# Attention keys turned by VectorE where they are normed, and loaded from DRAM already turned

## The chip, the cores and the metric

The kernel runs on one core of a Trainium2 chip. The time is that of the device, in microseconds, from runs of the whole program; the profile and the trace come from one profiled execution. The engines are called as in the profile: PE (TensorE, with PEld for its weight loads), DVE (VectorE), ACT (ScalarE), POOL (GpSimd) and SP (SyncE, which here issues nearly all DMAs). Each engine runs its instructions in the order in which they were written for it; a waiting instruction holds up all behind it on its engine.

## What is computed

One layer of a decoder: 1024 tokens, width 1024, float32. Half of the mixer is attention with eight heads in two key groups, over compressed, selected and windowed keys; the other half is a gated short convolution. A squared-ReLU MLP follows.

```python
h = rms_norm(x, g_mix_norm[l])
z = h @ w_in[l]
q, kc, vc, ks_, vs_, kw_, vw_, gl, hc, cg, bg = jnp.split(z, offs, axis=-1)
...
k_slc = rms_norm(ks_.reshape(kv_shape), g_k[l, 1])
k_win = rms_norm(kw_.reshape(kv_shape), g_k[l, 2])
...
attn_out = nsa_attention(q, k_cmp, v_cmp, k_slc, vs_.reshape(kv_shape),
                         k_win, vw_.reshape(kv_shape), gates)
conv_out = short_conv_mixer(hc, cg, bg, conv_w[l])
mixed = jnp.concatenate([rms_norm(attn_out, g_out[l, :ATTN_WIDTH]),
                         rms_norm(conv_out, g_out[l, ATTN_WIDTH:])], axis=-1)
x = x + mixed @ w_o[l]
h = rms_norm(x, g_ffn_norm[l])
x = x + jnp.square(jax.nn.relu(h @ w_up[l])) @ w_down[l]
```

The change concerns `k_slc` and `k_win`, the selected and the windowed keys: 1024 tokens by two groups of 64 each.

## The kernel before

**One plan for all engines.** Every operation is first recorded in a `Plan`. A list scheduler with a table of costs then puts the records of each engine in an order, the table `MOVES` sets some of them ahead of others by hand, and only then are they written out, all by one helper line (L268). So the order on an engine is not that of the source, and a record more or less renumbers those behind it: `MOVES` names records by number. `plan.drag` multiplies the size that the scheduler reckons for a DMA.

**Precision.** Products are built from float32 numbers split in two: a rounded high part and the rest, as in `KH` and `KL` for the keys, `hTh` and `hTl` for activations, `wcuh` and `wcul` for weights. ACT makes the high part and DVE or POOL the low one.

**Stages in time.** Norms and transposes of the input (0 to 28 us); products with the columns of `w_in` for keys, values, queries and gates (`zp`, to 150 us) with the compression MLP between (`hp`); convolution channels (`zX`, `zZ`, `zW`, 141 to 264 us), a Strassen-like scheme; the product with `w_o` for the convolution half (`wc`, from 264 us), with which the first scores (`s_`) are interleaved; attention (to 590 us); the MLP (`Z`, `X`, `W`, `Y`, to the end).

**The keys.** `k_norm(src, br, tb)` runs for each of eight token blocks and two branches: branch 1 (selected) from 31 to 73 us, branch 2 (windowed) from 134 to 157 us. DVE norms a block into `krow` (128 tokens by two groups by 64), and SP stores it twice, side by side, into `k_d[br]`, which lies in DRAM by tokens, in 256-byte pieces. At 257 us SP loads it back in four loads `kn`. `k_transposes` then turns it on PE: 32 transposes `tp<-ident,kn` into eight PSUM tiles. `split_keys` makes `KH` from each tile on ACT and `KL` on DVE, with the keys' 64 dimensions along the partitions, as the scores need them. `KH[g]` holds the high parts of a group twice, in both halves of the partitions; `KL` holds the low parts of both groups. Half of the transposes stand ahead of the `wc` groups, the others between them.

**Buffers.** `krow` comes from the pool `zt` with two buffers. A tile of the third k_norm waits until the first one's stores have landed. The weights of the convolution stage come in loads `wcr`, which ACT scales by the norm's gain (`wcr<-wcr,cols`, four pieces) and splits (`wcuh`); DVE makes `wcul`. Before the change the first `w_o` weights, residual rows (`y3`, `y2`, ...), `kn`, queries (`qx`) and values (`vs`, `vw`) are loaded between 256 and 275 us.

## Time and profile before

| | |
|---|---|
| median of 3 runs | 1213.78 us (1213.2 to 1215.11) |
| span of the profiled execution | 1212.3 us, 1.5 us below the median |
| PE busy | 1202.0 us, 99% of the span |
| 32 transposes of keys | 266.4 to 290.7 us, 272 ns median duration |
| eight `KH` and eight `KL` operations from PSUM | 598 and 688 ns median |
| `krow` stores | 32, 64 KB each, 586 ns of SP each, landing after 2.3 us (median) |
| DVE busy, 125 to 150 us | 22.30 of 25 us |
| DMA, 260 to 275 us | 354 to 372 GB/s |

A profile row of the timeline gives the start, the duration, the engine, the operation with its output and inputs, and in brackets the idle time ahead of it with what ended it. A duration on PE is a latency: matmuls follow one another more closely, 0.23 us for 512 columns and about 0.11 us for 128. What the engine spends is read from the distance between starts.

### The profile page before, as it was taken

To read this page: it belongs to the slowest core of one execution; us is meant where nothing else is said; L and a number is where in the kernel's file an instruction comes from. 1 tells how busy PE (TensorE), PEld (TensorE's weight loads), DVE (VectorE), ACT (ScalarE), POOL (GpSimd) and SP (SyncE) were. 2 spreads that over 40 slices of the span, in tenths; PEclk is the share of its full clock that TensorE was granted. 3 is DMA by queue.
4 is the path that set the end of the run, shared out by engine and by line. 5 is a ranking of instruction groups with operands and counts; after the bars stand their busy time and mean duration, and the time that the engine had idled before them with its cause. 6 is when DMAs were issued, how large, how long until landed. Compare 5 with 4: busy or idle time off the path is not lost.

```text
span 1212.3 us, 18361 instructions
## 1 busy us (share of the span) xinstructions
PE 1202.0 (99%) x5991; PEld 997.8 (82%) x5991; DVE 917.1 (76%) x1786; ACT 719.7 (59%) x1586; POOL 707.2 (58%) x629
## 2 busy tenths in 40 slices
PE   9999999999999999999999999999999999999998
PEld 6888977778888888888788888888888888888887
DVE  7957867684787898988866556555658898888885
ACT  7577855551588888778856556455335444444441
POOL 2444400011255545335859877777789999989971
PEclk9999999999999999999999999999999999999999
DMA  6375522265121200002234553535539555543513
GB/s 249 79 206 168 169 77 52 60 206 178 42 82 36 70 20 17 28 18 71 87 122 155 176 173 122 182 109 171 190 138 401 163 167 166 177 145 113 175 51 139
DMA packets 104360, 156.06 MB, mean 129 GB/s; under 512 B 20229, under 2 KB 58457, under 8 KB 104265
## 3 DMA queue, kind: packets, MB, share of 16 engines
q1 hardware_dynamic: 98000, 147.06, 37.0%
q10 hardware_dynamic: 5496, 5.28, 1.3%
q0 software_dynamic: 768, 2.56, 0.7%
q8 instruction: 47, 0.77, 0.3%
q14 instruction: 49, 0.39, 0.1%
HBM read 106.63 MB, written 48.23 MB: 128 GB/s over the span
## 4 chain that ended last, share of the span: by engine, by line
PE 93%; ACT 3%; DVE 3%; DMA 1%; issue 1%; POOL 0%; ACTq 0%; DVEq 0%; POOLq 0%
PE X L268 28%; PE Z L268 18%; PE zp L268 9%; PE tp L268 6%; PE zX L268 5%; PE ot L268 5%; PE wa L268 4%; PE W L268 4%; PE wc L268 3%; PE zZ L268 3%; PE zW L268 1%; PE hp L268 1%; ACT ph L268 1%; ACT wu L268 1%; PE tpq L268 0%
## 5 line engine op out<-in xcount | busy, mean ns | idle before, releaser
L268 PE MATMUL X<-we,uu 128*128 128x512 f32 x720 | 202.3, 389 | 0.0
L268 PE MATMUL Z<-we,uu 128*128 128x512 f32 (+1 forms) x582 | 169.1, 387 | 0.0
L268 PEld LDWEIGHTS X<-we,uu 128*128 128x128 f32 x720 | 135.1, 188 | 28.1
L268 ACT ACTIVATE uu<-ur 128x512 fp32r<-128x512 f32 x108 | 66.5, 630 | 116.8 <-PE Z L268 58.3
L268 PEld LDWEIGHTS Z<-we,uu 128*128 128x128 f32 x582 | 108.6, 188 | 22.4
L268 ACT ACTIVATE pt<-pt,nm 128x640 f32<-128x640 f32 (+7 forms) x128 | 93.7, 735 | 17.5 <-DVE nm L268 17.5
L268 PE MATMUL tp<-ident,pt 128*128 128x128 f32 x528 | 102.4, 272 | 0.2
L268 DVE TENSOR_TENSOR y<-X,y 128x512 f32<-128x512 f32 x128 | 86.2, 684 | 20.6 <-PE X L268 20.1
L268 POOL TENSOR_TENSOR d<-d 128x512 f32<-128x512 f32 x64 | 96.1, 1522 | 9.6 <-DVE d L268 7.5
L268 DVE TENSOR_TENSOR pl<-tp,ph 128x512 fp32r<-128x512 f32 (+1 forms) x148 | 94.7, 653 | 7.3 <-ACT ph L268 6.9
L268 ACT ACTIVATE ph<-tp 128x512 fp32r<-128x512 f32 (+1 forms) x148 | 82.4, 575 | 28.5 <-PE tp L268 26.0
L268 DVE TENSOR_TENSOR y<-Z,y 128x512 f32<-128x512 f32 (+1 forms) x97 | 65.3, 679 | 27.1 <-PE Z L268 26.9
L268 POOL TENSOR_TENSOR uu<-ur,uu 128x512 fp32r<-128x512 f32 x54 | 82.3, 1530 | 0.9 <-ACT uu L268 0.7
L268 PEld LDWEIGHTS tp<-ident,pt 128*128 128x128 f32 x528 | 68.5, 140 | 10.5 <-POOL pt L268 0.6
L268 DVE TENSOR_TENSOR we<-s,we 128x512 fp32r<-128x512 f32 x42 | 41.2, 982 | 47.5 <-PE Z L268 19.0
L268 ACT ACTIVATE we<-s 128x512 fp32r<-128x512 f32 x55 | 34.7, 631 | 65.0 <-PE Z L268 36.5
L268 ACT ACTIVATE we<-wu 128x512 fp32r<-128x512 f32 x57 | 36.1, 636 | 54.4 <-PE X L268 39.7
L268 POOL TENSOR_TENSOR we<-wd,we 128x512 fp32r<-128x512 f32 x32 | 52.1, 1628 | 25.1 <-ACT we L268 24.9
L268 POOL IOTA d_sw<- 128x640 f32 (+1 forms) x2 | 1.2, 610 | 107.9 <-PE zZ L268 107.9
L268 DVE TENSOR_TENSOR we<-wu,we 128x512 fp32r<-128x512 f32 x38 | 49.2, 1297 | 18.2 <-PE X L268 9.9
L268 PE MATMUL zp<-w_lo,hTh 128*128 128x512 f32 (+1 forms) x192 | 62.9, 363 | 0.0
L268 POOL TENSOR_TENSOR pt<-pt,rr 128x640 f32<-128x640 f32 (+4 forms) x64 | 62.3, 1004 | 0.0
(1337 smaller groups left out, 3738.3 us busy)
## 6 DMA issues: line engine op xcount, KB each, us to landing
u_d<-d SPq DMA_DIRECT2D x112, 256.0 KB, 4.0
ur<-u_d SPq DMA_DIRECT2D x108, 256.0 KB, 2.8
wu<-in_w_up_dram SPq DMA_DIRECT2D x16, 1024.0 KB, 5.9
wd<-in_w_down_dram SPq DMA_DIRECT2D x16, 1024.0 KB, 7.0
xt<-in_x_dram SPq DMA_DIRECT2D x10, 512.0 KB, 5.4
w_raw<-in_w_in_dram SPq DMA_DIRECT2D x8, 512.0 KB, 5.3
w1r<-in_w_cmp_dram SPq DMA_DIRECT2D x16, 256.0 KB, 2.9
q_d<-qn SPq DMA_DIRECT2D x8, 512.0 KB, 5.1
```

Of the source, the lines that this page charges most:

```text
L268: getattr(engine, method)(*[real(x) for x in a], **{k: real(x) for k, x in kw.items()})
```

## The change

`k_norm` makes the split and the turn itself. ACT copies `krow` rounded into the first half of `kn`, POOL subtracts for the second half, and one DVE instruction turns the 128x256 tile in blocks of 32x32 into `kT`. Four stores, one for each 32 tokens, put it into `k_d[br]`, which now lies by dimension: 128 rows of high parts and 128 of low ones, 1024 tokens in a row. A store moves 32 KB in 256 pieces of 128 bytes. `kn` and `kT` have two buffers each.

Gone are the four loads of `kn`, the 32 transposes, and the eight operations each on ACT and DVE. In their place stand 20 loads on SP: 16 of 64x512 into the halves of `KH`, four of 128x512 into `KL`. The loads of `V` now stand behind them in the source. `MOVES` is renumbered, and has 22 entries fewer, 87 instead of 109; those that are gone name records of the first 350 us. [...]

```diff
-    k_d = [dram.tile([T, G * 2 * HD], F32, name=f"k_d{br}") for br in range(2)]
+    k_d = [dram.tile([2 * P, T], F32, name=f"k_d{br}") for br in range(2)]
...
-            kd = k_d[br - 1][tb * P:(tb + 1) * P].rearrange("p (g a d) -> p g a d", g=G, a=2)
-            for a in range(2):
-                nc.sync.dma_start(kd[:, :, a], dst)
+            kn = zt.tile([P, 2, G * HD], F32R, name="kn")
+            kT = zt.tile([P, 8, 32], F32, name="kT")
+            row = dst.rearrange("p g d -> p (g d)")
+            copy_act(kn[:, 0], row)
+            tt(nc.gpsimd, kn[:, 1], row, kn[:, 0].bitcast(F32), ALU.subtract)
+            nc.vector.transpose(kT.rearrange("p c i -> p (c i)"), kn.rearrange("p a n -> p (a n)").bitcast(F32))
+            kd = k_d[br - 1].rearrange("(c j) t -> j c t", j=32)
+            plan.drag = 2.7
+            for a in range(4):
+                t = tb * P + 32 * a
+                nc.sync.dma_start(kd[:, :, t:t + 32], kT[32 * a:32 * a + 32])
+            plan.drag = 1.0
...
-        kn = {}
-        for qd in range(2):
-            for br in range(2):
-                kn[br, qd] = y_tile([P, 4, G, 2 * HD], f"kn{br}{qd}")
-                nc.sync.dma_start(kn[br, qd].rearrange("p t g d -> p t (g d)"),
-                                  k_d[br][qd * 512:(qd + 1) * 512].rearrange("(t p) n -> p t n", p=P))
...
+        for qd in range(2):
+            for br in range(2):
+                t = slice(qd * 512, (qd + 1) * 512)
+                c = slice(NCMP + br * T + qd * 512, NCMP + br * T + (qd + 1) * 512)
+                for g in range(G):
+                    for h_ in half:
+                        nc.sync.dma_start(KH[g][h_, c].bitcast(F32), k_d[br][half[g], t])
+                nc.sync.dma_start(KL[:, c].bitcast(F32), k_d[br][P:, t])
...
-        def k_transposes(g, br, qd):
-            tp = psP.tile([P, 4, P], F32, name="tp", tag="pt")
-            for j in range(4):
-                nc.tensor.transpose(tp[:, j], kn[br, qd][:, j, g], ident)
-            c0 = NCMP + br * T + qd * 512
-            split_keys(g, c0, 512, tp.rearrange("p a b -> p (a b)"))
...
-        kts = [(i % 2, i // 2 % 2, i // 4) for i in range(8)]
-        for i in range(4):
-            k_transposes(*kts.pop(0))
...
-            for i in range(2):
-                if kts:
-                    k_transposes(*kts.pop(0))
...
-    nc = _bacc.Bacc("TRN2", target_bir_lowering=False, num_devices=1)
+    nc = _bacc.Bacc("TRN2", target_bir_lowering=False, num_devices=1, dynamic_dma_scratch_size=8192)
```

**Where the order moves, first place: the convolution stage at about 161 us.** PE, before; the numbers behind names are those of records, and `wcuh_2213` and `wcul_2217` are the weight tile that the product `zX_2078` opens with:

```order
L268 MATMUL zW_2005<-hTh0_173,wcul_2046 128x512
L268 MATMUL zX_1882<-hTh1_124,wcul_2156 128x512
L268 MATMUL zZ_1972<-hTh1_124,wcuh_2152 128x512
L268 MATMUL zZ_1972<-hTl1_123,wcuh_2152 128x512
L268 MATMUL zZ_1972<-hTh1_124,wcul_2159 128x512
L268 MATMUL zZ_1972<-hTh1_124,wcuh_2152 128x512
L268 MATMUL zZ_1972<-hTl1_123,wcuh_2152 128x512
L268 MATMUL zZ_1972<-hTh1_124,wcul_2159 128x512
L268 MATMUL zX_2078<-hTh0_173,wcuh_2213 128x512
```

The same place of PE after the change, where that tile is `wcuh_2305` with `wcul_2329`:

```order
L268 MATMUL zW_2108<-hTh0_173,wcul_2134 128x512
L268 MATMUL zX_1994<-hTh1_124,wcul_2180 128x512
L268 MATMUL zX_2175<-hTh0_173,wcuh_2305 128x512
L268 MATMUL zX_2175<-hTl0_172,wcuh_2305 128x512
L268 MATMUL zX_2175<-hTh0_173,wcul_2329 128x512
L268 MATMUL zX_2175<-hTh0_173,wcuh_2305 128x512
L268 MATMUL zX_2175<-hTl0_172,wcuh_2305 128x512
L268 MATMUL zX_2175<-hTh0_173,wcul_2329 128x512
L268 MATMUL zX_2175<-hTh0_173,wcuh_2305 128x512
L268 MATMUL zZ_2066<-hTh1_124,wcuh_2251 128x512
```

ACT at the same place, before:

```order
L268 ACTIVATE ca_2171<-zZ_1972 128x512
L268 ACTIVATE wcuh_2209<-wcr_1731 128x512
L268 ACTIVATE wcr_2182<-wcr_2182,cols_64 128x256
L268 ACTIVATE wcuh_2213<-wcr_1732 128x512
L268 ACTIVATE wcr_2182<-wcr_2182,cols_64 128x256 x3
```

And ACT after the change, with the last `kn` copy of k_norm ahead:

```order
L268 ACTIVATE wcuh_2251<-wcr_1767 128x512
L268 ACTIVATE kn_2208<-krow_2196 128x128
L268 ACTIVATE wcuh_2298<-wcr_1767 128x512
L268 ACTIVATE wcr_2232<-wcr_2232,cols_64 128x256 x4
L268 ACTIVATE wcuh_2305<-wcr_1768 128x512
```

The six `zZ` matmuls that stood between the products now stand behind, and all four scalings of the load `wcr_2232` stand ahead of the tile that the `zX` product opens with.

**Second place: DVE ahead of it, about 150 to 156 us.** Before:

```order
L268 SCALAR_TENSOR_TENSOR krow_1978<-z_1962,kri_1873,gk_bc_169 128x64 x2
L268 TENSOR_TENSOR wcul_2046<-wcr_1731,wcuh_2033 128x512
L268 TENSOR_TENSOR hTl1_123<-ta_1934,hTh1_124 128x512
L268 SCALAR_TENSOR_TENSOR krow_2009<-z_1999,kri_1961,gk_bc_169 128x64 x2
L268 TENSOR_SCALAR gates_63<-ge_1856 128x12
```

After, where `wcul_2134` is the tile that was `wcul_2046`:

```order
L268 STREAM_TRANSPOSE kT_2071<-kn_2034 128x256
L268 TENSOR_TENSOR tb_2016<-hTl1_123 128x512
L268 TENSOR_SCALAR rs_t_2003<-kss_1996 128x2
L268 SCALAR_TENSOR_TENSOR krow_2073<-z_2045,kri_1986,gk_bc_169 128x64 x2
L268 TENSOR_TENSOR ta_2060<-ta_2060,tb_2016 128x512
L268 SCALAR_TENSOR_TENSOR krow_2112<-z_2097,kri_2044,gk_bc_169 128x64 x2
L268 STREAM_TRANSPOSE kT_2136<-kn_2102 128x256
L268 TENSOR_TENSOR hTl1_123<-ta_2060,hTh1_124 128x512
L268 STREAM_TRANSPOSE kT_2162<-kn_2143 128x256
L268 TENSOR_SCALAR gates_63<-ge_1886 128x12 x2
L268 TENSOR_SCALAR rs_t_2057<-kss_2049 128x2
L268 TENSOR_TENSOR wcul_2134<-wcr_1767,wcuh_2124 128x512
```

The weight tile stood between two k_norms; now two block transposes, the fifth and the sixth of this branch, and the rows between them stand ahead of it.

**Third place: SP at about 257 us.** Before:

```order
L268 DMA kn00_3024<-k_d0_194 128x4x256
L268 DMA kn10_3025<-k_d1_193 128x4x256
L268 DMA kn01_3026<-k_d0_194 128x4x256
L268 DMA y3_3028<-in_x_dram 128x1024
L268 DMA kn11_3027<-k_d1_193 128x4x256
L268 DMA y2_3029<-in_x_dram 128x1024
L268 DMA qx_3041<-q_d_197 128x512
L268 DMA vs_3048<-v_ds_192 128x8x256
```

After:

```order
L268 DMA y3_3136<-in_x_dram 128x1024
L268 DMA y2_3137<-in_x_dram 128x1024
L268 DMA KH0_3158<-k_d0_194 64x512 x2
L268 DMA KL_3156<-k_d0_194 128x512
L268 DMA KH0_3158<-k_d1_193 64x512 x2
L268 DMA KL_3156<-k_d1_193 128x512
L268 DMA y1_3138<-in_x_dram 128x1024
L268 DMA qx_3153<-q_d_197 128x512
L268 DMA KH1_3157<-k_d0_194 64x512 x2
L268 DMA vs_3160<-v_ds_192 128x8x256
```

The loads go straight into `KH` and `KL`, and the first of them wait for the last matmuls of the convolution stage, whose operands lay in that memory. From 352 us on PE has the same order as before, and from 165 to 256 us all engines have nearly the same.

More of the change, by code (lines that the diff above doesn't have):

```diff
@@ L1140, in trunk_layer @@
         V = {br: vp.tile([P, NT, G, 2, HD], F32R, name=f"v{br}", tag=f"v{br}") for br in "sw"}
-        kn = {}
-        for qd in range(2):
-            for br in range(2):
-                kn[br, qd] = y_tile([P, 4, G, 2 * HD], f"kn{br}{qd}")
-                nc.sync.dma_start(kn[br, qd].rearrange("p t g d -> p t (g d)"),
-                                  k_d[br][qd * 512:(qd + 1) * 512].rearrange("(t p) n -> p t n", p=P))
-        for br in "sw":
-            nc.sync.dma_start(V[br].rearrange("p t g a d -> p t (g a d)").bitcast(F32),
-                              v_d[br].rearrange("(t p) n -> p t n", p=P))
         kp_stack = ExitStack()
@@ L1159, in split_keys @@
             tt(nc.vector, KL[half[g], c0:c0 + n], ps[half[g]], KH[g][half[g], c0:c0 + n].bitcast(F32), ALU.subtract)
+        for qd in range(2):
[6 more added lines that the diff above has]
+                nc.sync.dma_start(KL[:, c].bitcast(F32), k_d[br][P:, t])
+        for br in "sw":
+            nc.sync.dma_start(V[br].rearrange("p t g a d -> p t (g a d)").bitcast(F32),
+                              v_d[br].rearrange("(t p) n -> p t n", p=P))
         d_sw = kp.tile([P, 1152], F32, name="d_sw")
```

41 rows, old and new, of the table MOVES are left out of this document.

## The prediction

> **What bounds the kernel now.** I read the page first (busy time, then the chain of work that ended last), then the timeline around the key transposes, then the tiles that the change touches.
>
> ```profile
> span 1212.3 us, 18361 instructions
> PE 1202.0 (99%) x5991; PEld 997.8 (82%) x5991; DVE 917.1 (76%) x1786; ACT 719.7 (59%) x1586; POOL 707.2 (58%) x629
> PE 93%; ACT 3%; DVE 3%; DMA 1%; issue 1%; POOL 0%; ACTq 0%; DVEq 0%; POOLq 0%
> ```
>
> TensorE (PE) is busy in 99% of the span and owns 93% of the chain. So a matmul taken away is time gained one to one, unless PE stands still beside it, and a stall added to PE is time lost one to one. What the other engines do counts only where PE then waits. The median of the runs, 1213.78, is 1.5 us above this execution's span; I take those 1.5 us as lying around it and unchanged, and add all changes to the median.
>
> **The change, part by part.**
>
> *1. The 32 PE transposes go.* The stage where they stand:
>
> ```profile
> 266.36 1.03 PE L268 MATMUL tp<-ident,kn 128*128 128x128 f32 x8
> 267.15 0.48 PE L268 MATMUL wc<-hTl,MCh 128*128 128x512 f32 x1
> ...
> 269.53 0.40 PE L268 MATMUL wc<-hTl,MCh 128*128 128x512 f32 x1
> 270.17 0.50 PE L268 MATMUL wc<-hTl,MCh 128*128 128x512 f32 x1 [0.25 <-DVE hTl L268]
> ...
> 271.21 0.40 PE L268 MATMUL wc<-hTl,MCh 128*128 128x512 f32 x1
> 271.98 0.50 PE L268 MATMUL wc<-hTh,MCh 128*128 128x512 f32 x1 [0.37 <-DVE KL L268]
> ```
> ```profile
> 286.25 1.15 PE L268 MATMUL tp<-ident,kn 128*128 128x128 f32 x9
> 287.26 0.50 PE L268 MATMUL wc<-hTh,MCh 128*128 128x512 f32 x1
> ```
>
> Starts, not durations, show the cost of a pipelined matmul: 8 transposes from 266.36 to 267.15 (0.099 us each), 9 from 286.25 to 287.26 (0.112 us). 32 at 0.108 are **-3.5 us**. Nothing else runs on PE beside them, so the whole is on the path.
>
> *2. Waits of PE in that stage go.* Two `wc` matmuls normally start 0.23 us apart. 269.53 to 270.17 is 0.41 too long, 271.21 to 271.98 is 0.54; together 0.95, with a small one behind them about 1.1 us, and the releaser is DVE.
>
> ```profile
> 265.00:270.00 5.00, 4.93 (x28) 3.85 (x26) 4.96 (x9) 3.01 (x5) 3.19 (x6) 1.00 1.06 372
> 270.00:275.00 5.00, 4.46 (x17) 3.08 (x18) 4.50 (x8) 1.58 (x4) 0.00 (x0) 1.00 1.10 354
> ```
> ```profile
> L268 ACT ACTIVATE KH<-tp x8: 582/598/602, 270.0 to 290.9; 128x512 fp32r<-128x512 f32 x8
> L268 DVE TENSOR_TENSOR KL<-tp,KH x8: 672/688/695, 271.2 to 291.5; 64x512 fp32r<-64x512 f32 x8
> ```
>
> These windows give the length, then busy time of PE, PEld, DVE, ACT and POOL, the clock, the DMA share and GB/s. DVE is full (4.96 of 5), and four of the eight `KL` subtractions (0.69 us each) stand here. Without them and the `KH` copies on ACT the chain to `hTl` ends before PE comes: **-1.1 us**. PE itself arrives up to 1.3 us earlier (twelve transposes less), so some of it can come back; evacuations into `y3` are then next in line, and a third query block `qx` now stands behind ten more loads on SP. I put **+0.7** for these (0 to 1.5: from nothing to two waits as long as the two above plus half a one).
>
> *3. What the 20 key loads cost.*
>
> ```profile
> 264.09 0.39 PE L268 MATMUL zX<-t4h,wcul 128*128 128x512 f32 x1
> 264.32 0.61 PE L268 MATMUL wc<-hTh,MCh 128*128 128x512 f32 x2
> ```
>
> They bring 3 MB, against 2 MB in four loads, into a stretch where the queues already carry 354 to 372 GB/s (rows above, last number). They can start when the matmuls that read the memory under `KH` are done, about 264.3. The first score then stands 71 `wc` matmuls behind (before: 105 and the 32 transposes): 264.3 + 71 x 0.23 = 280.6 at the earliest. The first 1 MB at 360 GB/s, with the residual rows ahead of it, takes 4 to 7 us: landed by 272. Cost **0**, covered by 8 us of `wc` matmuls; without that cover each us late is a us lost.
>
> *4. Scores begin earlier.* Softmax work on DVE and ACT starts about 34 matmuls (7.7 us) sooner against the rest. From 320 to 350 PE's starts lie some 2.4 us further apart in all than without waits; the two rows with a releaser, and the fullest window (columns as above):
>
> ```profile
> 326.87 0.39 PE L268 MATMUL s__3648<-KH,Qg 128*128 128x256 f32 x1 [0.26 <-DVE nm L268]
> 345.76 0.50 PE L268 MATMUL ot<-pl,vw 128*128 128x512 f32 x1 [0.34 <-DVE pl L268]
> ```
> ```profile
> 330.00:340.00 10.00, 9.88 (x66) 8.16 (x65) 9.95 (x22) 8.39 (x19) 6.00 (x8) 1.00 0.28 81
> ```
>
> DVE is full there (9.95 of 10), so a head start on it is worth something. Bounds 0 to -2.4. From 352 us on PE's order is that of before, so a head start can be spent only here. I take **-0.7**.
>
> *5. What k_norm adds.* Sixteen times: an ACT copy, a POOL subtraction, a DVE transpose 128x256 and two more stores. No row shows the block transpose; nearest is the DVE copy of the same shape, 0.42 us, between a `krow` product (0.28) and a 128x512 subtraction (0.69).
>
> ```profile
> 126.00 0.42 DVE L268 COPY hT<-tp 128x256 f32<-128x256 f32 x1 [0.32 <-PE tp L268]
> ```
> ```profile
> L268 DVE SCALAR_TENSOR_TENSOR krow<-z,kri,gk_bc x32: 272/278/590, 35.2 to 154.9; 128x64 f32<-128x64 f32 x32
> L268 SPq DMA_DIRECT2D k_d<-krow x32: 513/586/652, 38.8 to 156.4; - x32
> ...
> DMA to landing us min/median/max: 1.9/2.3/5.1
> ```
>
> [...]
>
> ```profile
> 50.00:75.00 25.00, 25.00 (x109) 20.15 (x108) 16.27 (x37) 15.82 (x52) 10.84 (x15) 1.00 0.81 211
> ...
> 125.00:150.00 25.00, 25.00 (x184) 23.96 (x184) 22.30 (x61) 20.52 (x84) 12.07 (x14) 1.00 0.65 185
> ```
> ```profile
> 136.33 0.68 DVE L268 SCALAR_TENSOR_TENSOR krow<-z,kri,gk_bc 128x64 f32<-128x64 f32 x2 [0.44 <-POOL kri L268]
> ```
> ```profile
> L268 POOL TENSOR_TENSOR vrow<-z,vrow x16: 456/703/2851, 30.6 to 154.4; 128x128 fp32r<-128x128 f32 x16
> ```
>
> The first eight (31 to 82 us) fall where DVE has room (16.27 of 25 us busy from 50 to 75); by the order the query weights stand behind two more rows (0.7 us) and are used five matmuls later (5 x 0.23): **0**. The second eight (136 to 158 us) are the danger. DVE is busy 22.30 of 25 us there, and its transposes stand in one row with the `wcul` weight tiles that PE takes just in time. A transpose waits for its `kT` buffer, that is for the landing of four stores issued two k_norms earlier. By hand: the first `krow` is there at 136.9, the ACT copy and the POOL subtraction (0.5 to 0.7, by `vrow`, which has its shape) need about 1.5 us, and with the rows that stand ahead of them on DVE transposes 1 and 2 come at 139.1 and 143.0, each followed by 4 x 0.586 = 2.3 us of issue and 2.3 of landing; the fourth at 149.0, its stores issued 150.2 to 152.6 and landed 154.4; the sixth then 154.4, and `wcul_2134` behind it done at 155.8. PE needs it at 155.9:
>
> ```profile
> 155.91 0.40 PE L268 MATMUL zW<-hTh,wcul 128*128 128x512 f32 x1
> ...
> 161.05 0.39 PE L268 MATMUL zZ<-hTh,wcuh 128*128 128x512 f32 x1
> ...
> 162.44 0.39 PE L268 MATMUL zX<-hTh,wcuh 128*128 128x512 f32 x1
> ```
> ```profile
> 160.57 0.63 ACT L268 ACTIVATE wcuh<-wcr 128x512 fp32r<-128x512 f32 x1 [3.48 <-PE zW L268]
> 161.19 0.51 ACT L268 ACTIVATE wcr<-wcr,cols 128x256 f32<-128x256 f32 x1
> 161.61 0.61 ACT L268 ACTIVATE wcuh<-wcr 128x512 fp32r<-128x512 f32 x1
> 162.13 1.29 ACT L268 ACTIVATE wcr<-wcr,cols 128x256 f32<-128x256 f32 x3
> ```
>
> So no stall there, but no reserve either. The stall comes **at 161 us**, by order. Before, six `zZ` matmuls with a weight tile long ready cover 161.05 to 162.44 while ACT makes the next tile. Now the `zX` product comes first, and its `wcuh_2305` stands on ACT behind `wcuh_2298` (free when a `zW` matmul ends, 160.57) and four scalings of a weight load. 160.57 + 0.52 + 4 x 0.43 + 0.6 = 163.4: PE, ready at 161.05, stands 2.4 us. If the load lands later, more:
>
> ```profile
> 157.14 0.56 SPq L268 DMA_DIRECT2D wcr<-in_w_in_dram  x1
> ```
> ```profile
> L268 SPq DMA_DIRECT2D wcr<-in_w_in_dram x20: 367/499/1087, 129.1 to 220.9; - x20
> ...
> DMA to landing us min/median/max: 2.9/3.8/5.6
> ```
>
> That load now stands behind the sixth k_norm's stores: transposed 154.8, stores 156.0 to 158.3, load issued 158.7, landed 162.5, tile at 164.9: 3.9 us. Bounds 2.4 (stores issued at 0.33) and 9.5 (landings of 5.1 us, below); I take **+3.1**, between the floor and the hand chain.
>
> Sum: -3.5 - 1.1 + 0.7 - 0.7 + 3.1 = **-1.5 us**, 1213.78 - 1.5 = **1212.3**.
>
> **Rivals.**
>
> *Faster.* The stall at 161 stays at its floor, 2.4, `y3` and `qx` cost nothing, and the early scores take all of the 2.4 us: -3.5 - 1.1 - 2.4 + 2.4 = -4.6, **1209.2**. For it speaks that ACT and DVE lose 4.8 and 5.5 us of `KH` and `KL` work right ahead of the softmax; against it, that 320 to 350 us is also short of ACT.
>
> *Slower.* The stores of 128-byte pieces land late and DVE, held at a `kT` buffer, holds the weight tiles behind it. Two landings lie in a row on the chain above (second to fourth, fourth to sixth k_norm). At 5.1 us (the longest row above) instead of 2.3 the sixth transpose comes 5.6 us later, `wcul_2134` makes PE wait 5, and the tile at 161 is 3.9 + 5.6 = 9.5 us late: -3.5 - 1.1 + 9.5 = +4.9, **1218.7**. It ends on the slow side (+2.4, a stall of 7.0) from a landing of 2.3 + (7.0 - 3.9) / 2, about 3.9 us, on.
>
> ```profile
> k_d<-krow SPq DMA_DIRECT2D x8, 64.0 KB, 2.0
> v_dw<-vrow SPq DMA_DIRECT2D x2, 128.0 KB, 1.7
> ```
>
> Half the bytes in pieces a quarter as long land 0.3 us later here; for a 32 KB store in 128-byte pieces that speaks for about 2.3, not 5. [...]
>
> *It does not do what it says.* The twelve transposes at 266 to 268 may only have filled PE time that would have been waiting for `hTl` anyway. Then 20 transposes count (2.2 us), and part 2 brings nothing: -2.2 + 0.7 - 0.7 + 3.1 = +0.9, **1214.7**. DVE's lost `KL` work speaks against it.
>
> **How the numbers follow.** A measurement of this kernel tells about 0.2% from no change, 2.4 us: 1211.4 to 1216.2. Forecast 0.36 (all of it within), no effect 0.10 (within), faster 0.36, slower 0.18. Together faster 0.36, same 0.46, slower 0.18. The forecast's own range is 1211.0 to 1214.0. To hold 8 in 10 the range reaches most of the faster case (1209.2, with the spread of its terms 1208.5) and the nearer third of the slower one, which begins at 1216.2 and whose price stands at 1218.7: 1217.0. Outside are then 0.12 above and some 0.06 below.
>
> **What would show it.** PE should have no `tp<-ident,kn` rows and no wait for DVE at 270 to 272. At 161 us (PE time of before) a `zX` matmul should wait for ACT `wcuh`, 2.4 to 3.9 us: no wait there and part 5 is wrong. A `zW` matmul waiting for DVE `wcul` near 156 and a DVE transpose idle for `k_d<-kT` speak for the slower rival, as does a `k_d<-kT` landing of about 4 us or more. Fewer idle rows of PE from 320 to 350 speak for the faster one. A score waiting for `KH` loads after 280 us would make part 3 wrong.

## The result, and the profile after

| | before | changed |
|---|---|---|
| median of the runs | 1214.44 us (1213.2 to 1215.47) | 1224.75 us (1224.4 to 1226.65) |
| span of the profiled execution | 1212.3 us | 1224.9 us |

The ratio of the runs is 1.0091, with a 95% interval of 1.0076 to 1.0105: about 10.3 us slower, where 1.5 us faster was forecast. The profiled execution of the changed kernel is the slowest of its four, so its trace shows some 2 us more than the median does. One execution of another kernel, the traced one of one_store_right_keys (last row of the table further down), took 1331 us at a granted clock of 0.85 and is counted in no ratio. The page after:

```profile
span 1224.9 us, 18389 instructions
PE 1201.4 (98%) x5959; PEld 995.4 (81%) x5959; DVE 919.2 (75%) x1794; ACT 717.7 (59%) x1594; POOL 719.0 (59%) x645
PE 84%; DMA 4%; DVE 4%; ACT 4%; issue 2%; SPq 1%; POOL 1%; ACTq 0%; DVEq 0%; POOLq 0%
```

PE lost its 32 transposes (x5991 to x5959), but its share of the chain fell from 93 to 84%, and SP's queue, which was not in the chain at all, has 1%. What PE waits for in the first 400 us (total, times, longest):

```profile
PE wc L268 <- DVE y L268: 2.4, 3, 1.6
PE zX L268 <- ACT wcuh L268: 2.2, 1, 2.2
PE zp L268 <- ACT z L268: 1.8, 2, 1.0
...
PE zX L268 <- ACT ta L268: 1.4, 1, 1.4
PE tp L268 <- DMA rows<-in_pe_cmp_dram: 1.3, 1, 1.3
PE hp L268 <- ACT w1h L268: 1.0, 1, 1.0
PE tp L268 <- DMA ch<-kv_d: 0.8, 1, 0.8
```

And all that PE waited for before, from 60 to 180 us:

```profile
PE hp L268 <- DVE w1l L268: 0.6, 1, 0.6
PE hp L268 <- ACT w1h L268: 0.4, 1, 0.4
```

To see where the time goes, the table further down takes the same matmul in each trace (the n-th that writes a tile of that name) and gives how much later it starts than in the trace of before; the times at the head of the columns are those of before. The changed kernel is 0.8 us late at 50 us, 2.8 at 128, 6.9 at 150, 11.6 at 176 (the end of the zp and zX stages), stays there to 264, gains 2.0 by 326 (end of the wc stage), loses 2.2 again by 372 (first softmax blocks) and ends 12.2 late. From 128 to 150 us (to 157 in its own trace), PE's rows with a releaser, and ACT and SP at the same place (start, length, engine, operation):

```profile
143.08 0.40 PE L268 MATMUL zp<-w_hi,hTh 128*128 128x280 f32 x1 [0.75 <-ACT z L268]
146.16 0.39 PE L268 MATMUL zp<-w_hi,hTh 128*128 128x280 f32 x1 [1.02 <-ACT z L268]
147.83 0.55 PE L268 MATMUL zX<-hTh,wcuh 128*128 128x512 f32 x1 [0.63 <-ACT z L268]
```
```profile
141.71 0.51 ACT L268 ACTIVATE wcr<-wcr,cols 128x256 f32<-128x256 f32 x1 [3.67 <-DMA wcr<-in_w_in_dram]
142.12 0.61 ACT L268 ACTIVATE wcuh<-wcr 128x512 fp32r<-128x512 f32 x1
142.64 0.38 ACT L268 ACTIVATE z<-zp 128x280 f32<-128x280 f32 x1
```
```profile
137.85 0.34 SPq L268 DMA_DIRECT2D v_dw<-vrow  x1
138.24 0.43 SPq L268 DMA_DIRECT2D wcr<-in_w_in_dram  x1
```

Read from below: a weight load stands on SP behind a store of V and goes out at 138.24, when that store could. The store waited for POOL, which made its `vrow` from 137.37 to 137.83. No store of keys stands ahead of it here: the first one of this branch is issued at 145.72. ACT, which takes its work in order, stands 3.67 us before the scaling of that load, and the copy `z<-zp`, which frees the tile in PSUM that PE writes next, stands behind it. PE waits three times, 2.40 us in all, and then something follows that no row with a releaser shows (windows: length, busy PE, PEld, DVE, ACT, POOL, granted clock, DMA share, GB/s):

```profile
147.00:148.00 1.00, 0.37 (x3) 0.17 (x2) 1.00 (x6) 0.93 (x6) 0.81 (x2) 1.00 0.90 239
148.50:149.00 0.50, 0.50 (x4) 0.50 (x4) 0.50 (x2) 0.50 (x4) 0.50 (x2) 0.50 0.46 75
```

For 3.41 us from 148.1 on the granted clock is 0.50: PE looks full, but its `zp` matmuls of 280 columns start 0.23 us apart in this stretch and 0.13 behind it. By the clock that is half of the stretch, another 1.7 us of this execution (an estimate), and with the 2.4 us of waits it makes up the 4.1 us that are lost from 128 to 150.

The stall that the forecast put "at 161 us" is there, 2.2 us at 169.8 of this trace, with just the row on ACT that it named, four scalings ahead of the tile `wcuh`:

```profile
169.53 0.63 ACT L268 ACTIVATE wcuh<-wcr 128x512 fp32r<-128x512 f32 x1 [2.57 <-PE zW L268]
170.06 1.69 ACT L268 ACTIVATE wcr<-wcr,cols 128x256 f32<-128x256 f32 x4
171.66 0.61 ACT L268 ACTIVATE wcuh<-wcr 128x512 fp32r<-128x512 f32 x1
```

And the tile `kT`, over the whole run (ns min/median/max, first and last start; landing in us):

```profile
L268 SPq DMA_DIRECT2D k_d<-kT x64: 302/444/1617, 53.6 to 169.7; - x64
L268 DVE STREAM_TRANSPOSE kT<-kn x16: 429/446/447, 53.1 to 167.5; 128x256 f32<-128x256 f32 x16
  DMA k_d<-kT: 3.2, 2
DMA to landing us min/median/max: 1.5/1.7/4.4
```

A block transpose takes 0.446 us (0.42 was taken), and a store's landing has a median of 1.7 us (1.5 to 4.4), below the 2.3 of the old stores. Two of the slower rival's signs do show: DVE stands twice for a landing (third line, 3.2 us in all), and the longest landing is over 4 us. But both lie in the first branch, the waits at 70.16 us (1.36) and 81.89 us (1.80). In the second branch, where the rival had its price, no transpose waits for a landing and no `zW` matmul for a `wcul`. So stores that land late are not what made the time, though it came out on that rival's side.

### The profile page after: what moved, and what is told of

Same layout as the page of the kernel before. It is cut to its first block, busy times and chain, and to the rows that moved or that the text cites. A ratio compares the mean times of both kernels' runs of the same rounds, so it can differ in the third digit from the quotient of the medians.

```text
span 1224.9 us, 18389 instructions
## 1 busy us (share of the span) xinstructions
PE 1201.4 (98%) x5959; PEld 995.4 (81%) x5959; DVE 919.2 (75%) x1794; ACT 717.7 (59%) x1594; POOL 719.0 (59%) x645
## 4 chain that ended last, share of the span: by engine, by line
PE 84%; DMA 4%; DVE 4%; ACT 4%; issue 2%; SPq 1%; POOL 1%; ACTq 0%; DVEq 0%; POOLq 0%
PE X L268 28%; PE Z L268 18%; PE zX L268 6%; PE tp L268 5%; PE ot L268 5%; PE W L268 4%; PE wa L268 4%; PE zZ L268 3%; PE zp L268 3%; PE wc L268 2%; SPq L268 1%; DMA xt<-in_x_dram 1%; PE zW L268 1%; DMA w1r<-in_w_cmp_dram 1%; DMA w_raw<-in_w_o_dram 1%
## 5 line engine op out<-in xcount | busy, mean ns | idle before, releaser
L268 PE MATMUL zp<-w_hi,hTh 128*128 128x512 f32 (+1 forms) x192 | 62.3, 368 | 1.8 <-ACT z L268 1.8
```

The source lines that it names most:

```text
L268: getattr(engine, method)(*[real(x) for x in a], **{k: real(x) for k, x in kw.items()})
```

## Experiments

These theories were held against each other as they came up. A: the change itself costs little, and the loss is the 22 hand-made moves (of 109) that the changed kernel no longer has. B: the work added to k_norm on DVE, ACT and POOL costs it; E is B for ACT alone. C: the stores hold DVE at the kT buffers. D: four issues a block fill SP's queue, and weight loads behind them come late. F: the key loads get their memory late and push the loads behind them. G: DVE is late there because softmax rows come sooner. H: the softmax stage, where DVE is full, takes back what the transposes gave. O: only the order is wrong.

| run | ratio to before, 95% | late at 50 | 128 | 176 | 264 | 326 | 372 | end |
|---|---|---|---|---|---|---|---|---|
| changed kernel | 1.0091 (1.0076, 1.0105) | 0.8 | 2.8 | 11.6 | 11.6 | 9.6 | 11.8 | 12.2 |
| before_less_moves | 1.0012 (1.0003, 1.0022) | 0.8 | -0.4 | 0.2 | 0.4 | 1.0 | 0.7 | 0.6 |
| after_less_two_moves | 1.0060 (1.0045, 1.0075) | 0.8 | 2.2 | 7.6 | 7.7 | 5.4 | 7.2 | 8.0 |
| after_start_and_less_two | 1.0060 (1.0045, 1.0075) | 0.5 | 2.2 | 6.7 | 6.7 | 4.9 | 7.1 | 7.1 |
| wcr_load_first | 1.0046 (1.0023, 1.0069) | 0.3 | 2.1 | 5.4 | 5.4 | 3.5 | 5.5 | 6.2 |
| one_store | 1.0044 (1.0029, 1.0058) | 0.3 | -1.2 | 2.1 | 2.2 | -0.5 | 1.6 | 3.1 |
| copy_not_waiting | 1.0063 (1.0040, 1.0085) | 0.2 | 2.0 | 6.3 | 6.3 | 4.5 | 6.6 | 7.5 |
| v_loads_first | 1.0047 (1.0025, 1.0070) | 0.0 | 2.2 | 8.0 | 8.0 | 4.2 | 6.2 | 6.6 |
| after_one_store | 1.0093 (1.0076, 1.0110) | 0.7 | 1.2 | 8.4 | 8.4 | 5.6 | 7.7 | 7.9 |
| both_moves | 1.0038 (1.0026, 1.0050) | 0.1 | 1.5 | 4.8 | 4.9 | 1.1 | 3.4 | 3.6 |
| both_moves_two_queues | 1.0075 (1.0060, 1.0090) | 0.4 | 1.8 | 8.9 | 9.1 | 5.4 | 7.6 | 8.9 |
| loads_alone | 1.0025 (1.0016, 1.0034) | 0.3 | 0.3 | 0.4 | 0.6 | 0.1 | 2.2 | 2.5 |
| loads_in_old_order | 1.0045 (1.0032, 1.0058) | 0.1 | 0.6 | 0.8 | 1.0 | 7.9 | 7.6 | 7.9 |
| loads_spread_old_order | 0.9999 (0.9989, 1.0009) | 0.3 | 0.6 | 0.6 | 0.8 | 0.1 | -0.2 | 0.3 |
| change_in_old_order | 1.0149 (1.0133, 1.0164) | 0.2 | 8.6 | 14.4 | 14.3 | 19.5 | 19.3 | 19.7 |
| change_spread_old_order | 1.0103 (1.0088, 1.0118) | 0.3 | 6.6 | 13.1 | 13.5 | 11.8 | 11.5 | 13.1 |
| one_store_right_keys | 1.0130 (1.0113, 1.0147) | | | | | | | |

Lateness is in us, by one trace each; the last run has no trace that can be laid beside the others. Stretches at half the clock fell into some of these executions: one of 3.41 us into the changed kernel, after_less_two_moves, v_loads_first, both_moves_two_queues and change_spread_old_order, 10.24 us into loads_in_old_order (mean clock 0.996), 13.65 in three places into change_in_old_order (0.994). So 1.7 us between two rows of the table can be that alone, and more in the last two; a verdict needs the ratio too. The traced execution is also not always the median one: that of the changed kernel is the slowest of its four, those of one_store and after_one_store are the fastest of theirs, 1.8 and 2.3 us under the median. Where the intervals of two rows overlap, as those of most single steps below do, the runs alone do not settle the step, and it rests on the waits in the traces.

**1. The hand-made moves.**

```diff
-        ((2080,), 2139), ((2081,), 2139), ... 22 moves, taken out of before
```


> The kernel before, with the 22 of its 109 hand-made moves taken out that the changed kernel no longer has; nothing of the keys is changed. Theory A (the change itself costs little; what it lost is the hand order that it could not keep): this kernel is slower than before by 8 to 13 us, with waits of the matrix engine near 140 and 161 us, and the changed kernel stands 1 to 4 us below it. Theory B (the added work in k_norm, on VectorE, ScalarE, GpSimd and the issuing queue, costs the time): this kernel is within 2.5 us of before and the changed kernel 8 us or more above it. Theory C (the new stores hold VectorE at the kT buffers): as B.

Measured: 1.4 us (0.12%). Theory A falls as worded: the lost moves are worth little in the plan that they were made for.

```diff
-        ((2083,), 1751), ((2204,), 2382),
```


> The changed kernel without two of its 87 moves: the one that puts the second load of wcr_1767 behind the v_dw store, and the one that puts wcuh_2298 ahead of the four wcr_2232 scalings. Theory A: the wait of 2.3 us at 169.8 us goes, and of the 3.6 us lost at 142 to 147 us most goes, so the time falls by 4 to 6 us against the changed kernel, with new waits elsewhere of up to 1.5 us. Theory B and C: under 1.5 us, since what was queued behind the added work only waits elsewhere.

Measured: 1224.75 to 1221.36 us, 3.4 of the 10.3, just under the expected 4 to 6. The wait of 142 to 147 us all but went (PE is 2.1 us late at the last zp in place of 6.9). Two of the moves that were kept did harm in the new plan, then; a move says "this ahead of that", and what stands between the two had changed. The wait for `wcuh` did not go with the second of them: 1.5 us stayed, since the load in front of it now came late (2. below).

```diff
+        ((402, 410, 411,), 207), ((188,), 395), ((187,), 181), ((186,), 180), ((103,), 178),
```


> As the run before, and five of the dropped moves put back, all on the first 20 us (which x transposes stand ahead of which first matmuls). Theory A: 0.8 us less than the run before, all of it lost before 20 us into the span. Theory B and C: no difference, since k_norm only begins at 39 us; here they expect under 0.3 us either way.

Measured: no difference in the runs (1221.46 against 1221.36). The trace is 0.3 us earlier at 50 us, and level with its parent's again at 113 us.

**2. What fills the queues: SP or ACT?** From 136 to 163 us, in the kernel of the last run:

```profile
157.93 1.90 SPq L268 DMA_DIRECT2D k_d<-kT  x4
159.92 0.39 SPq L268 DMA_DIRECT2D v_dw<-vrow  x1
160.42 0.40 SPq L268 DMA_DIRECT2D wcr<-in_w_in_dram  x1
```
```profile
164.55 1.71 ACT L268 ACTIVATE wcr<-wcr,cols 128x256 f32<-128x256 f32 x4 [2.18 <-DMA wcr<-in_w_in_dram]
```

Four stores and one more stand ahead of a weight load, and ACT then waits 2.18 us for that load.

```diff
+        ((2381,), 1914),
```


> The kernel of the run after_start_and_less_two with one move more: the load of wcr that SP issued at 160.42 us stands ahead of the four key stores that it issued from 157.93 us. Every other engine's order is as it was. Theory D (the four stores of each key block fill SP's queue, and a weight load behind them comes late): the load goes out 2 to 2.5 us sooner, the wait of 1.8 us at 165.2 us goes, and the kernel is 1.5 to 2.5 us faster than that run. Theory E (ScalarE's added copies and its waits for krow are what is late there): under 0.5 us.

Measured: the load goes out at 157.93, ACT's scalings start at 162.15 without a wait, and the `zX` wait falls from 1.8 to 0.6 us. 1221.46 to 1219.82 us: 1.6, as D expected, and 1.3 in the traces at 176 us; the intervals of the two ratios overlap. It did not win the whole wait, since ACT's next tile then waited 0.99 us for a `zW` matmul.

```diff
-            for a in range(4):
-                nc.sync.dma_start(kd[:, :, t:t + 32], kT[32 * a:32 * a + 32])
+            ks = k_d[br - 1][32 * tb:32 * tb + 32].rearrange("(c r) (q i) -> (r q) c i", r=4, i=32)
+            nc.sync.dma_start(ks, kT)
```


> As after_start_and_less_two, with one store of a key block (all 128 partitions, pieces of 128 bytes as before) where there were four; the order of all engines is the same. The keys land in other places of k_d, so the scores are computed from keys in wrong places. Theory D: SP's 1.84 us for the four issues fall to under 0.8 us, and what stands behind them (loads of wcr, the q and v stores) goes out sooner: 2.5 to 5 us faster than that run, all of it before 176 us. Theory E: under 1 us.

(The diffs of this and of some later runs show what is issued. In the kernel the records of the plan keep their places, and only what they issue is exchanged, so that the order stays the same.) Its `kT` rows from 130 to 172 us:

```profile
L268 DVE STREAM_TRANSPOSE kT<-kn x8: 431/446/449, 138.6 to 159.5; 128x256 f32<-128x256 f32 x8
L829 SPq DMA_DIRECT2D k_d<-kT x8: 359/371/452, 139.1 to 160.0; - x8
```

One store of 128 KB in pieces of 128 bytes takes SP 0.37 us to issue, where each of the four of 32 KB takes 0.44 (and each of the two of 64 KB before 0.59): in these the time does not go by the byte. With 1.4 us a block given back, PE is 4.6 us earlier at 176 us in the traces; the runs say 2.4 (1221.46 to 1219.02), just under D's range, the intervals of the two ratios overlap, and the trace is that of the fastest execution. So D is right in its sign, and its size is known only to between 2 and 5 us. Where it lies is not where D looked for it: 3.4 of the 4.6 us are gained by 128 us, in the first branch, and only 1.2 behind it, where the `wcuh` wait falls from 1.8 to 0.6 us, just as it did in wcr_load_first. The run also speaks against theory B as the main cause. All the added work on ACT, POOL and DVE is still in it, and yet it is ahead of before by 1.2 us at 128 and 0.6 at 150; only the 2.7 us lost from 150 to 176 are left for B. The same edit in the changed kernel itself:

> The changed kernel itself, all of its moves kept, with one store of a key block (128 partitions, pieces of 128 bytes) where it has four; nothing else differs in any engine's order. The keys land in other places of k_d, so the scores are computed from keys in wrong places. Theory D (the four issues fill SP's queue): the lateness against before at the end of the zX matmuls, 11.6 us in the changed kernel, falls by 4 to 8 us, and the time by as much. Rival (the lost order alone, or the added work on the other engines): under 1.5 us.

Measured: 3.2 us less late at 264 us, but 1224.3 us in the runs, level with 1224.75, with its four executions spread over 5 us. As worded, this is a miss for D, and the trace says why:

```profile
PE zX L268 <- ACT wcuh L268: 2.2, 1, 2.2
PE zp L268 <- ACT z L268: 1.7, 2, 1.0
PE zX L268 <- ACT ta L268: 1.4, 1, 1.4
```

The waits from 140 us on are those of the changed kernel to 0.1 us. Of the 3.2 us, 1.6 are gained by 128 us; the rest is about the 1.7 us of the half-clock stretch, which this execution does not have. So the four stores are not what PE waits for from 128 to 176 us in the changed kernel. They cost it something between 50 and 128 us: there the eight traced planned kernels with four stores in that branch lose 1.4 to 2.2 us on before, and the two with one store lose 0.5 and gain 1.5. DVE's waits for landings (3.2 us in the changed kernel) lie there too, and how long they are with one store is not shown, so C is not told apart from D in that branch; from 136 us on C has no wait to show in the changed kernel.

```diff
-            copy_act(kn[:, 0], row)
+            copy_act(kn[:, 0], gk_bc.rearrange("p b d -> p (b d)")[:, :P])
```


> As after_start_and_less_two, but ScalarE's copy into kn reads a constant tile in place of the key row, so that it never waits for VectorE (3.0 us of ScalarE's idle time stands ahead of these copies between 137 and 163 us); its 0.30 us of work stays. The high parts of the keys are replaced by constants, so the scores are not the reference's. Theory E: 2 to 4 us faster than that run, before 176 us. Theory D: under 0.7 us.

Measured: 1221.99 against 1221.46 us, no gain (0.4 in the traces at 176 us). ACT's waits for the key rows cost next to nothing here, and that half of theory E falls; the copies themselves, 0.30 us each, are still there. (The scores are not spoilt as expected: the subtraction takes off what the copy wrote, so the high and the low part still add up to the key.)

**3. The read side.** In the same kernel DVE stands still for a residual row, and PE for DVE:

```profile
295.35 1.41 DVE L268 SCALAR_TENSOR_TENSOR xt<-wc,rconv,xt 128x512 f32<-128x512 f32 x2 [2.75 <-DMA xt<-in_x_dram]
296.68 0.74 DVE L268 SCALAR_TENSOR_TENSOR y<-wc,rconv,y 128x512 f32<-128x512 f32 x1
```

```diff
+        ((3065, 3066,), 3045),
```


> As after_start_and_less_two, with the two loads of V ahead of the first load of the key tensors on SP, where that queue stood still from 264.4 to 271.2 us. Theory F (the key loads come late, because their buffers come free late, and push V, y and xt together, so xt lands at 295.4 us and VectorE stands still for it 2.75 us): the wait of 1.75 us at 297.5 us falls under 0.5 us and the kernel is 1 to 2.5 us faster than that run. Theory G (VectorE is late there because of softmax rows that come sooner): under 0.4 us.

Measured: the xt rows start at 293.88 without a wait, `y` on PE falls from 2.5 to 0.8 us, and from 264 to 326 us this kernel gains 3.8 us where its parent gains 1.8. 1.2 us in the runs, with overlapping intervals. Theory F holds by the trace, and G falls: the key loads wait for their memory (in the parent SP stands from 264.4 to 271.2 us ahead of the first), and what is issued behind and beside them comes late.

> The kernel of after_start_and_less_two with both moves of the second set: the wcr load ahead of four key stores, and the V loads ahead of the key loads; it computes the reference. Theories D and F, if they add: 2.5 to 3.5 us faster than after_start_and_less_two, so 3 to 4.5 us slower than before. If the one gain takes the place of the other: 1.5 us.

Measured: 1218.17 us, 3.3 below after_start_and_less_two, where 1.6 and 1.2 were gained one by one: the two gains add.

```diff
-                nc.sync.dma_start(kd[:, :, t:t + 32], kT[32 * a:32 * a + 32])
+                (nc.gpsimd if br == 2 and a > 1 else nc.sync).dma_start(kd[:, :, t:t + 32], kT[32 * a:32 * a + 32])
```


> As both_moves, with two of the four stores of each block of the second branch (those of 110 to 163 us) issued by GpSimd's queue in place of SP's; it computes the reference. Theory D: SP's issues shrink by 0.9 us a block and the time by 1 to 2.5 us against both_moves, if GpSimd (busy 0.5 to 0.85 of that stretch) has room for its issues. If GpSimd becomes late in their place (its pow for kri, its subtraction for kn): 0 to 4 us slower.

Measured: 1223.27 us, 5.1 slower than both_moves, in an order that the planner made anew for it, and beyond the 4 us that the rival allowed. The order changed with the queue, so this does not tell what issuing on GpSimd costs; as planned, it is no way out.

```diff
-    k_d = [dram.tile([2 * P, T], F32, name=f"k_d{br}") for br in range(2)]
+    k_d = [dram.tile([T, G * 2 * HD], F32, name=f"k_d{br}") for br in range(2)]
+    k_r = [k_d[br].rearrange("(a r) n -> a (r n)", r=4) for br in range(2)]
...
-                        nc.sync.dma_start(KH[g][h_, c].bitcast(F32), k_d[br][half[g], t])
+                        nc.sync.dma_start(KH[g][h_, c].bitcast(F32), k_r[br][half[g], t])
```


> The kernel before with its own key rows and stores (two of a block, as before), but with the 20 loads of the changed kernel straight into KH and KL, from k_d read as 256 rows of 1024, and without the 32 transposes and the 8 key splits behind them; the keys are in wrong places. All moves of before that still apply are kept (105 of 109). By the steps of the prediction (transposes gone, VectorE's waits gone, loads hidden, scores sooner): 3.5 to 5 us faster than before. Theory H (the wait for xt and y behind the late loads takes about 2 us, and the softmax stage from 326 to 372 us, where VectorE is busy 10.6 to 12 of every 12 us, gives about 2 us back): the matrix engine is 1.5 to 3.5 us ahead of before at 326 us, and only 0 to 1.5 us ahead at 372 us and at the end.

Measured: 3 us slower than before (0.25%), with nothing added to k_norm. This is the run that the forecast's parts 1 to 4 speak of: they add up to 4.6 us faster. PE waits 1.7 us for `qx` and 1.5 for `y`, and loses 2.1 from 326 to 372 us, as every version here does that has the planner's new order.

Next, every engine's order was written out as it is in before, so that on PE, DVE, ACT and POOL nothing but the removed rows differs:

```diff
     def moved(self, order):
-        for block, before in self.MOVES:
+        place = dict.fromkeys((n.k for n in order), -1)
+        place.update((k, i) for i, k in enumerate(SEQ))
```


> As loads_alone (before's key rows and stores, key loads straight into KH and KL, no transposes, keys in wrong places), with every engine in the order of before, less the rows removed. Theory O: 3 to 5 us faster than before, and the 2.1 us that loads_alone lost from 326 to 372 us is gone. Theory H: 2 to 3.5 us ahead at 326 us, and 0 to 1.5 us ahead at 372 us and at the end.

> As loads_in_old_order, with the key loads cut in two groups on SP: the ten of the first 512 tokens behind the y1 load as before, the other ten behind the y5 load, so that the xt load, which was issued at 284.7 us behind twenty key loads and for which VectorE stood still 7.9 us, stands ahead of them. Theory O (the read side gains once no queue holds it up): the wait of 6.9 us goes, the matrix engine is 2.5 to 4.5 us ahead of before at 326 us and still ahead by 2 to 4.5 us at the end. Theory H: ahead at 326 us, and level with before within 1 us at 372 us and at the end. Rival: the buffers of the key tensors come free too late for any order, so a wait of over 2 us stays.

Measured: with all twenty key loads in one place the xt load goes out at 284.67 us, DVE stands 7.90 us for it and PE 6.94 for DVE, and 10.24 us at half the clock follow from 288.5 us on, 4.2 of them while PE still stands; with ten of them behind the last x load, the kernel takes the time of before: 0.9999 (0.9989 to 1.0009). The 2.1 us from 326 to 372 us are gone in both (-0.3 us each), so that loss goes with the planner's order and not with a full VectorE alone: H falls, O holds there. But O also expected 2 to 4.5 us of gain at 326 us, and there are 0.7. PE's rows with a releaser in loads_spread_old_order, 262 to 326 us:

```profile
269.75 0.50 PE L912 MATMUL wc<-hTl,MCh 128*128 128x512 f32 x1 [0.57 <-DVE hTl L912]
271.01 0.50 PE L912 MATMUL wc<-hTl,MCh 128*128 128x512 f32 x1 [0.76 <-DVE hTl L912]
282.68 0.50 PE L912 MATMUL wc<-hTh,MCh 128*128 128x512 f32 x1 [0.22 <-DVE y L912]
286.58 0.50 PE L912 MATMUL wc<-hTh,MCh 128*128 128x512 f32 x1 [0.84 <-DVE y L912]
290.59 0.50 PE L912 MATMUL wc<-hTh,MCh 128*128 128x512 f32 x1 [0.28 <-DVE y L912]
293.52 0.50 PE L912 MATMUL wc<-hTh,MCh 128*128 128x512 f32 x1 [0.58 <-DVE xt L912]
```

These are 3.25 us where before has 0.80 in the same stretch (0.25, 0.37 and 0.18). The 3.5 us of transposes had filled PE while it would have waited for `hTl`, `y` and `xt`. That these come no sooner without the transposes and the key splits, the rows of DVE show, first in before, then in loads_spread_old_order:

```profile
269.38 0.74 DVE L268 SCALAR_TENSOR_TENSOR hTl<-wor,cols,hTh 128x512 fp32r<-128x512 f32 x1
271.25 2.11 DVE L268 TENSOR_TENSOR KL<-tp,KH 64x512 fp32r<-64x512 f32 x3
292.62 1.41 DVE L268 SCALAR_TENSOR_TENSOR xt<-wc,rconv,xt 128x512 f32<-128x512 f32 x2 [0.40 <-DMA xt<-in_x_dram]
```
```profile
270.22 0.74 DVE L912 SCALAR_TENSOR_TENSOR hTl<-wor,cols,hTh 128x512 fp32r<-128x512 f32 x1
292.72 1.41 DVE L912 SCALAR_TENSOR_TENSOR xt<-wc,rconv,xt 128x512 f32<-128x512 f32 x2 [2.18 <-DMA xt<-in_x_dram]
```

The second `hTl` row is 0.84 us later, as the whole stage is (0.8 at 264 us): the `KL` subtractions stood behind it on DVE, not ahead of it, so taking them out could not hasten it. The xt rows start at the same time in both, when their load has landed.

**4. The whole change in the old order, and one store with the keys right.**

> The whole change (all its operations, the keys right), but every engine's order is that of the kernel before, written out: the matrix engine's rows are those of before less the 32 transposes, and the new operations of a key block stand 0.3 us (copy), 1.2 us (subtraction), 2.2 us (block transpose) and 2.7 us (four stores) after the key row by the old plan's times; the 20 key loads stand behind the y1 load, the V loads where they were. Theory O (the change's loss lies in the orders that the planner found for it, above all on SP and ScalarE from 136 to 168 us and on SP and VectorE from 264 to 372 us): 0 to 4 us faster than before. Theory D (the stores' issues on SP cost 2 to 5 us whatever the order): 1 to 4 us slower than before, with waits from 142 to 170 us. Theory H (the softmax stage takes back what the transposes gave): the lead at 326 us is 2 to 3.5 us greater than that at 264 us, and is lost again by 372 us.

Measured: 19 us slower (some of it at half the clock: 13.65 us in this trace). SP and ACT at 60 us show what a waiting store does to the loads behind it:

```profile
51.85 0.39 SPq L1270 DMA_DIRECT2D v_ds<-vrow  x1
58.94 1.84 SPq L1270 DMA_DIRECT2D k_d<-kT  x4
60.82 0.97 SPq L1270 DMA_DIRECT2D w1r<-in_w_cmp_dram  x2
```
```profile
67.19 0.63 ACT L1270 ACTIVATE w1h<-w1r 128x512 fp32r<-128x512 f32 x1 [6.41 <-DMA w1r<-in_w_cmp_dram]
```

SP stands from 52.2 to 58.9 us for a block transpose on DVE with the w1r load behind it, and ACT then stands 6.41 us for w1r. This is not D, whose queue is full of issues; here the queue is held by one store whose data are not there yet.

> As change_in_old_order (the whole change, the reference computed), with the key loads in the two groups of the run before, and the new operations of each key block placed by the measured times of before: the copy 0.1 us, the subtraction 0.5 us, the block transpose 1.5 us and the four stores 2.8 us behind the end of the key row, so that SP should not stand still for a block transpose with weight loads behind it. Theory D (four issues of 0.46 us a block, 32 blocks' worth of 0.66 us more than before, in any order): 1 to 5 us slower at 176 us than before, level with before or up to 3 us slower at the end. Theory O: level within 1.5 us at 176 us, 1 to 4 us faster at the end.

Measured: 13 us slower, 13.1 late at 176 us. Later places for the stores helped by 2.0 us at 128 and 0.8 at 264 us; O's "level within 1.5 us at 176 us" is far off, and D's lateness is exceeded too. (There are 16 key blocks, not 32.) Neither of the two placings makes the old order a home for the new work. From 264 to 326 us it gains 1.7 and keeps that at 372.

```diff
+            ks = k_d[br - 1].rearrange("(c s) (j i) -> s j c i", c=8, i=32)[4 * tb:4 * tb + 4]
+            nc.sync.dma_start(ks.rearrange("a j c i -> (a j) c i"), kT)
...
-                        nc.sync.dma_start(KH[g][h_, c].bitcast(F32), k_d[br][half[g], t])
+                        for e in range(2): key_load(KH[g], h_.start + 32 * e, c, br, qd, 2 * g + e)
-                nc.sync.dma_start(KL[:, c].bitcast(F32), k_d[br][P:, t])
+                for e in range(4): key_load(KL, 32 * e, c, br, qd, 4 + e)
```


> The kernel of both_moves with one store of a key block (128 partitions, pieces of 128 bytes) into a k_d laid out so that the keys can be read back right: each load of KH is two loads and each of KL four, of 32 partitions in pieces of 128 bytes (48 loads where there were 20); the order is that of both_moves and the reference is computed. Theory D: at 264 us it stands 2.5 to 5 us below both_moves (4.9 us late there). If the 48 loads find room on SP, which is idle about half of 264 to 300 us, the end is 2 to 4.5 us faster than both_moves, level with before within 2 us. Rival: the loads in small pieces and 28 issues more come late, so xt, y and qx wait, and up to 6 us are lost from 264 to 326 us.

Measured: 1229.86 us, 11.7 slower than both_moves, so on the rival's side and past the 6 us that it allowed. Its trace cannot be laid beside the others, but has one sign for the rival: from 264 to 326 us PE waits 5.5 us for `qx`, for which it does not wait in both_moves. How the 11.7 us divide is not shown.

No version of the change tried beats the kernel before; both_moves, at 1.0038, is the nearest with the keys right.

## Why the prediction was wrong, point by point

- **Part 1, the transposes (-3.5).** The work went; the time did not. "Nothing else runs on PE beside them, so the whole is on the path" is the first step that failed. PE was busy there because the transposes filled the gaps: in loads_spread_old_order, which differs from before only in the key loads and in the transposes and splits left out, 0.7 us were gained from 264 to 326 us and 2.45 us of new waits appeared. The third rival ("it does not do what it says") had seen this for the first twelve transposes, at a chance of 0.10; that DVE's lost `KL` work speaks against it was the misreading of part 2.
- **Part 2, the waits at 270 us (-1.1, and +0.7 for new ones).** The 0.37 us for `KL` went; the wait for `hTl` did not (0.24 us in the changed kernel, 0.25 before). "Without them and the `KH` copies on ACT the chain to `hTl` ends before PE comes" misreads DVE's order: the `KL` rows start at 271.25 us, behind both `hTl` rows. PE's waits for `y` measured 2.4 us in the changed kernel, against the 0.7 put for new ones, the largest 1.6 behind a DVE row that waited for xt.
- **Part 3, the key loads (0).** Asked of the wrong side. No score waited for `KH` or `KL`. But xt, y and qx stood behind them on SP and in the DMA queues, and their readers waited: 2.64 us on DVE for xt in the changed kernel (median landing of the xt loads 7.4 us there, 3.6 before), 1.7 us on PE for qx in loads_alone.
- **Part 4, the early scores (-0.7).** The sign was wrong. The changed kernel loses 2.2 us from 326 to 372 us, where PE now waits 2.4 us and before 0.6. In the old order that loss is absent, so it lies in the order that the planner gives that stage. (The orders differ a little beyond 352 us, up to 357 on PE and 362 on DVE and ACT.)
- **Part 5, the first eight blocks (0).** The room was looked for on DVE. The changed kernel loses 2.0 us from 50 to 128 us; with one store a block 1.5 of these go. The price is on the side of the stores, and DVE's room did not cover it.
- **Part 5, the stall at 161 (+3.1).** Right in place and mechanism: 2.2 us, on the row of ACT named, by the floor's path (2.4) and without a late load.
- **Part 5, the hand chain (no other stall).** The second step that failed, and the largest: the changed kernel is 11.6 us late at 176 us, of which the forecast had 3.1. From 128 to 150 us 4.1 are lost, 2.4 in waits for ACT's `z` and 1.7 at half the clock; from 150 to 176 another 4.7, where beside the 2.2 foreseen PE waits 1.4 us for ACT's `ta`. The chain followed DVE's rows and the stores' landings. It did not ask which loads stood behind which stores on SP, of V as well as of keys, nor what ACT does when such a load is late. Taking out two moves that had been carried over gave 3.4 us, and setting one load ahead of four stores some 1.5 (1.6 in the runs, 1.3 in the traces).
- **The slower rival.** Its time (1218.7) and sign were nearer than the forecast's, its mechanism was wrong: landings got shorter (1.7 us in the median), smaller pieces or not, and the two waits for them fell at 70 and 82 us, not on the weight tiles. SP was named, but for the time that stores need to land and not for what its queue holds up. That it came nearer was luck.

What stays open: 4.5 us of both_moves. In its trace 4.9 us are lost by 264 us. By one_store the stores' issues can be up to some 3 of them, since that run's gain on the `wcuh` wait is already in both_moves. The largest single wait left, 1.4 us where `zX` waits for ACT's `ta` (162 us in the changed kernel), stands in every planned version of the change but one. In both_moves ACT is then at work without a gap on a `z`, two `vrow` and a `ksq` row that stand ahead of `ta`, while the last `zX` matmul that it can wait for started 4.9 us before; in before `ta` has its place ahead of such rows and PE does not wait. That points at ACT's order, but it was not tried by itself. Nor was the added work on POOL and DVE taken out alone.

## What to carry to other kernels

In loads_spread_old_order 3.5 us of rows taken from a full engine were worth 0.7 us, because the engine then waited in their place: before subtracting such a row, look for the loads and evacuations that arrive while it runs. When a change adds instructions to an in-order queue, list for each what stands behind it there and who waits for that; the harm came not to the stores, nor to the readers of the new loads, but to weight loads and residual rows queued behind them, or behind a store whose data were late. And an order tuned by hand for one set of instructions is not neutral for another: two of the moves that were carried over cost 3.4 us.

## What the runs showed of the hardware

- SP took 0.37 us to issue a store of 128 KB in 1024 pieces of 128 bytes (one_store), 0.44 for one of 32 KB in 256 such pieces (the changed kernel), and 0.59 for one of 64 KB in 256 pieces of 256 bytes (before; all medians): among these the time does not grow with the bytes, and the one large store took a fifth of what four small ones did (0.37 against 1.78).
- In the changed kernel the granted clock fell to 0.50 behind short waits of PE: three waits of 2.4 us in all, within 5.5 us and none over 1.02, are followed by 3.41 us at 0.50, which by the clock cost 1.7 us more than the waits show (an estimate). In after_one_store the same waits (2.34 us) are followed by none. In loads_in_old_order 10.24 us at 0.50 begin within a wait of 6.94 us. What brings such a stretch on is not shown. Kernels with such waits spread over 2 to 5 us from run to run (2.25 in the changed kernel, 4.62 in loads_in_old_order, 5.23 in after_one_store), where those of before stay within 2.4 of each other in one comparison; that the clock is the reason is argued, not shown.
